# One more pair of the up-projection by Strassen's scheme, and VectorE's taps and Silu product one step later

## The chip, the core and the metric

The kernel runs on one core of a Trainium2 chip (trn2). The metric is the device time of one execution in microseconds (us). Rows of the profile name the engines PE (TensorE's matmuls), PEld (its weight loads), DVE (VectorE), ACT (ScalarE), POOL (GpSimd) and SP (SyncE, which here only issues DMAs).

## The reference

A decoder layer on one sequence of 512 positions and 1024 channels: three mixers (a short convolution, block-sparse causal attention, attention to a fixed memory), a gated merge with a residual add, and then the MLP, in which the change lies:

```python
h2 = rmsnorm(x, g_ffn)
a, b = jnp.split(h2 @ w_up, 2, axis=-1)        # w_up: 1024 x (2 * 2816)
a = causal_dwconv3(a, ffn_conv_w, ffn_conv_b)  # three taps along the positions
x = x + (jax.nn.silu(a) * b) @ w_down
```

All inputs are float32.

## The kernel before

**Tiling.** Channels lie on the partitions in chunks of 128 and the 512 positions along the free axis. Every float32 operand of a matmul is split into a high part (`hi`, rounded by ScalarE) and the rest (`lo`, a subtraction on VectorE), and a product is three matmuls: hi x hi, lo x hi, hi x lo. The weights of the layer are read in pieces of 128 x 1024 in the order of their use.

**The up-projection** makes 22 pairs: columns f and 22 + f of `w_up` give one 128 x 512 block of `a` and one of `b`. Pairs 0 and 1 are made together in 16 steps. A *plain* pair (`plain_pair`, pairs 2 to 5) takes 8 steps of TensorE, each of 6 matmuls of 512 columns. A *fast* pair (`fast_head` and `fast_tail`, pairs 6 to 20, the set `FAST`) multiplies a 2 x 2 arrangement of weight blocks (two column blocks, two halves of the 1024 rows) by a 2 x 2 arrangement of the input (two halves of the rows, two halves of the positions) by Strassen's scheme in the form with fewer sums: 7 products, one step each, of 12 matmuls of 256 columns. The order is head of f (`p6`, `p7`, `p1`, `p5`), tail of f - 1 (`p4`, `p2`, `p3`), head of f + 1, and so on. Pair 21 is plain again and comes outside this list.

A fast pair needs sums of its weights and of the input. The weight sums `sx` are made by VectorE (`sums_1`, `sums_2`, `sums_4`, lines 1199, 1203, 1244), and one of them in place by a GpSimd DMA that adds r2 to r1 (line 1200). The split weights are called `wx` (128 x 1024, of `sx`), `w1` (of r1 after the DMA), `w2` (by DMA, below) and `w4` (128 x 512, of `sx`). The sums of the input (`sum_rows`, split by `sum_split` into the tiles `t`) are made once, at fixed steps ahead of the first fast pair.

**Drains.** The four banks of a pair are called y, z, x and w. ScalarE copies y (`p6_done`, line 1218) and a half of x (`p2_done`, line 1254). VectorE adds from x, z and w (`p1_done`, lines 1222 and 1223; `p5_done`, 1227; `p4_done`, 1250; `p3_done`, 1257). Even pairs use two banks `s` and two banks `m`, odd pairs four banks `acc`, so a bank is written again two pairs later. After `p3_done` come the three taps (`taps_of`): ScalarE the first (line 1074), VectorE the two others (line 1077), ScalarE Silu (line 1081), and VectorE the product with b (`gate_up`, lines 1087 and 1094). Pairs 14 to 17 (`SPILL`) write that product to DRAM by SP.

**Order.** In this stage the order on VectorE, ScalarE, SP and GpSimd is written out: `at(step, job)` puts a job in the list of a step, `later(gen)` runs a generator, one part a step, and every `yield` in it moves the rest to the next step. Jobs of a step run in the order in which they were put there, ahead of the step's matmuls; what drains a product runs behind them. Each engine then works through its own list in order, waiting at each instruction for what that instruction needs. `cut_at` plans a split: `high` at a step h, `low` one step later, h being the first use less a lead (`LEAD`, 7 steps); with `by_dma` ScalarE writes the negated high part as well and two GpSimd DMAs add the weights to it, in place of VectorE's subtraction. Splits go round six places (`place`, `ends`), three in the pool `wp` and three in `fs`; `ends` holds the step of the last use of each place.

Of the kernel before, what the change touches and what calls it, by code (L numbers as in the profile page):

```python
# [25 lines left out]
NWARM = 16  # L26


FAST = frozenset(range(6, 21))


LEAD = 7
# [35 lines left out]
def weight_units():  # L68
# [33 lines left out]
    for f in range(2, NF):  # L102
        if f in FAST:
            for ks in (range(4), range(4, KD)):
# [19 lines left out]
def layer_kernel(ctx: ExitStack, tc: tile.TileContext, xT, memT, vecs, ws, outT):  # L124
# [5 lines left out]
    wp = ctx.enter_context(tc.tile_pool(name="wp", bufs=3))  # L130
# [10 lines left out]
    def nm(s):  # L141
        count[0] += 1
        return f"{s}_{count[0]}"
# [3 lines left out]
    def tmp(n=S, dt=F32):  # L147

        i = tmps[0]
        if i is not None:  # L150
            tmps[0] = (i + 1) % 10
            if i >= 8:
                return cm.tile([P, n], dt, tag="tmp", name=nm("tmp"), bufs=2)
        return tp.tile([P, n], dt, tag="tmp", name=nm("tmp"), bufs=8)
# [3 lines left out]
    def bank(tag="acc"):  # L158
        return ps.tile([P, 512], F32, tag=tag, name=nm(tag), bufs=PSB[tag])
# [97 lines left out]
    def mm3(out, l, r, start, stop):  # L257
        nc.tensor.matmul(out, l[0], r[0], start=start, stop=False)  # L258
        nc.tensor.matmul(out, l[1], r[0], start=False, stop=False)  # L259
        nc.tensor.matmul(out, l[0], r[1], start=False, stop=stop)  # L260
# [14 lines left out]
    def split(dst, src, scale=None):  # L275

        for _ in split_steps(dst, src, scale):
            pass
# [615 lines left out]
    fs = fast.enter_context(tc.tile_pool(name="fs", bufs=1, reuse_waits="tile"))  # L894
# [3 lines left out]
    def taps(f):  # L898
        return [V("f_w", NF * i + f) for i in range(3)], V("f_b", f)
# [16 lines left out]
    def at(i, job):  # L916
        jobs.setdefault(max(i, now[0] + 1), []).append(job)

    def later(gen, wait=1):

        def go():
            if next(gen, "end") is None:
                at(now[0] + 1, go)

        if wait:
            at(now[0] + wait, go)
        else:
            go()
# [4 lines left out]
    base = st["cut"]  # L933
    done = {-1}
    PLACES = 6
    ends = [-1, -1, -1, -1, 3, 7]
    wanted = []
    cutn = [0]
    n_up = 2 * (NF - 2) + 2
# [29 lines left out]
    def place(n):  # L969

        i = cutn[0]
        cutn[0] = i + 1
        pool = fs if i % PLACES in (1, 2, 3) else wp
        return tuple(
            pool.tile([P, 8 * P], FR, tag=t, name=nm(t), bufs=3)[:, :n] for t in ("hi", "lo")
        )
# [35 lines left out]
    def cut_raw(i, first, last, by_dma=False, lead=LEAD):  # L1012
        return cut_at(first, last, lambda: raws[base + i], i, by_dma, lead)
# [9 lines left out]
    def blocks(hl, k, n=1):  # L1023
        return tuple(a[:, k * P : (k + n) * P] for a in hl)
# [45 lines left out]
    def taps_of(f, u, b):  # L1070

        ws, bias = taps(f)
        t = tmp()
        nc.scalar.activation(t, u[:, 0:S], AF.Identity, bias=bias, scale=ws[0])
        yield
        for i in (1, 2):
            nc.vector.scalar_tensor_tensor(
                t, u[:, i : S + i], ws[i], t, op0=ALU.mult, op1=ALU.add
            )
        yield  # L1080
        nc.scalar.activation(t, t, AF.Silu)
        yield
        gate_up(f, b, t)

    def gate_up(f, b, t):
        if f in SPILL:
            nc.vector.tensor_mul(t, b, t)
            nc.sync.dma_start(md[f], t)
            mf[f] = None
            return  # L1090
        n = sum(m is not None for m in mf.values())
        pool, tag = (fm, "mf") if n < NF - 8 - len(SPILL) else (mp, "mj")
        m = pool.tile([P, S], F32, tag=tag, name=nm("mf"))
        nc.vector.tensor_mul(m, b, t)
        mf[f] = m
# [21 lines left out]
    def sum_rows(k):  # L1117

        if k % 2 == 0:
            raw_sums[k] = [tmp() for _ in range(4)]  # L1120
        top, low, c = x2[k], x2[k + KH], slice(H * (k % 2), H * (k % 2) + H)
        t1, t2, t3, t4 = (r[:, c] for r in raw_sums[k & ~1])
        nc.vector.tensor_sub(t1, top[:, H:], top[:, :H])
        nc.vector.tensor_sub(t2, low[:, H:], t1)
        yield
        nc.vector.tensor_sub(t3, low[:, H:], top[:, H:])
        nc.vector.tensor_sub(t4, low[:, :H], t2)

    def sum_split(k, n):
        hl = tuple(fs.tile([P, S], FR, tag="t", name=nm("t"), bufs=16) for _ in range(2))  # L1130
        split(hl, raw_sums[k][n])
        sums[n].extend(tuple(a[:, H * i : H * i + H] for a in hl) for i in range(2))

    for k in range(KH):
        later_at = 24 + 8 * (k // 2) + 2 * (k % 2)
        at(later_at, lambda k=k: later(sum_rows(k), 0))
    for k in range(0, KH, 2):
        for n in range(4):
            at(28 + 4 * k + n, lambda k=k, n=n: sum_split(k, n))

# [3 lines left out]
    def plain_pair(f):  # L1146
        tags = ("acc", "acc") if f % 2 else ("s", "m")
        ws, bias = taps(f)
        box = {}

        def mms(w, h, j):
            def go():
                if j == 0:
                    box[h] = bank(tags[h])
                for k in (2 * j, 2 * j + 1):
                    mm3(box[h], blocks(w, k), hn[k], k == 0, k == KD - 1)

            return go

        def conv():  # L1160
            acc, t = box[0], tmp()
            box["t"] = t
            nc.scalar.activation(t, acc, AF.Identity, bias=bias, scale=ws[2])
            yield
            for i in (1, 2):
                nc.vector.scalar_tensor_tensor(
                    t[:, i:], acc[:, : S - i], ws[2 - i], t[:, i:], op0=ALU.mult, op1=ALU.add
                )
            yield
            nc.scalar.activation(t, t, AF.Silu)  # L1170

        for h in range(2):
            s = len(steps)
            by_dma = f < min(FAST) and (h == 1 or f < 4)
            w = cut_raw(2 * (f - 2) + 2 + h, s, s + 3, by_dma, LEAD + 4 if by_dma else LEAD)
            after = (lambda: later(conv(), 0), lambda: gate_up(f, box[1], box["t"]))[h]
            for j in range(4):
                steps.append((mms(w, h, j), after if j == 3 else None))
# [10 lines left out]
    def fast_head(f):  # L1189
        tags = ("acc",) * 4 if f % 2 else ("s", "m", "s", "m")  # L1190
        s = len(steps)
        i1 = 2 * (f - 2) + 2
        n = KH * P
        q = {}

        def sums_1():
            r1, r2 = raws[base + i1], raws[base + i1 + 1]
            q["sx"] = fs.tile([P, 2 * n], F32, tag="sx", name=nm("sx"), bufs=3)
            nc.vector.tensor_sub(q["sx"][:, n:], r1[:, :n], r1[:, n:])
            nc.gpsimd.dma_start(r1[:, n:], r2[:, n:], accum_op=ALU.add)  # L1200

        def sums_2():
            nc.vector.tensor_sub(q["sx"][:, :n], raws[base + i1 + 1][:, n:], q["sx"][:, n:])

        def sums_at(h):
            at(h - 2, sums_1)
            at(h - 1, sums_2)

        wx = cut_at(s, s + 1, lambda: q["sx"], known=sums_at)
        w1 = cut_raw(i1, s + 2, s + 3, lead=LEAD - 1)  # L1210

        def p6():
            q["y"], q["z"], q["x"], q["w"] = (bank(t) for t in tags)
            q["v"] = tmp()
            product(q["y"], wx, 0, sums[1], True)

        def p6_done():
            nc.scalar.activation(q["v"][:, :H], q["y"][:, :H], AF.Copy)

        def p1_done():  # L1220
            v = q["v"]
            nc.vector.tensor_add(v[:, H:], q["x"][:, :H], v[:, :H])
            nc.vector.tensor_add(v[:, :H], q["z"][:, :H], v[:, H:])

        def p5_done():
            q["b"] = tmp()
            nc.vector.tensor_add(q["b"][:, H:], q["w"][:, :H], q["v"][:, :H])

        steps.extend((
            (p6, p6_done),  # L1230
            (lambda: product(q["z"], wx, KH, sums[2], True), None),
            (lambda: product(q["x"], w1, 0, rows(0, 0), True), p1_done),
            (lambda: product(q["w"], w1, KH, sums[0], True), p5_done),
        ))
        return q
# [31 lines left out]
    for f in range(2, NF - 1):  # L1267
        this = (f, fast_head(f)) if f in FAST else plain_pair(f)
        if tail:
            fast_tail(*tail)  # L1270
        tail = this
    if tail:
        fast_tail(*tail)
    assert NF - 1 not in FAST and cutn[0] == 0
    end = len(steps)
# [17 lines left out]
    i = base + n_up - 2  # L1293
# [19 lines left out]
    for f in range(NF):  # L1313
        pool, tag = (fd, "m") if f < NF - 8 else (hp, "h")
# [83 lines left out]
```

## Time and profile before

| | us |
|---|---|
| median of 3 runs (827.23 to 827.34) | 827.24 |
| the profiled execution | 826.2 |
| its span in the trace | 824.4 |
| TensorE busy | 815.3 |
| VectorE busy | 569.7 |
| ScalarE busy | 436.3 |

The profiled execution took 826.2 us. Its span, from the first instruction of the program to the last, is 824.4; the rest lies around it. Busy time is the union of an engine's instructions. Matmuls overlap in the trace, so the time that one costs is the distance between two starts and not its length. In a timeline a row stands for one instruction, or for several of one kind in a row (x2); the brackets give the idle time of the engine ahead of it and what ended it. TensorE's granted clock is at its upper level (2.4 GHz) in all 40 slices of the profile.

### The profile page before, as it was taken

To read this page: it belongs to the slowest core of one execution; us is meant where nothing else is said; L and a number is where in the kernel's file an instruction comes from. 1 tells how busy PE (TensorE), PEld (TensorE's weight loads), DVE (VectorE), ACT (ScalarE), POOL (GpSimd) and SP (SyncE) were. 2 spreads that over 40 slices of the span, in tenths; PEclk is the share of its full clock that TensorE was granted. 3 is DMA by queue.
4 is the path that set the end of the run, shared out by engine and by line. 5 is a ranking of instruction groups with operands and counts; after the bars stand their busy time and mean duration, and the time that the engine had idled before them with its cause. 6 is when DMAs were issued, how large, how long until landed. Compare 5 with 4: busy or idle time off the path is not lost.

```text
span 824.4 us, 11450 instructions
## 1 busy us (share of the span) xinstructions
PE 815.3 (99%) x4254; PEld 695.0 (84%) x4254; DVE 569.7 (69%) x963; ACT 436.3 (53%) x779; POOL 95.7 (12%) x134
## 2 busy tenths in 40 slices
PE   9999999999999999999999999999999999999998
PEld 7888788888888888888888888899999998888888
DVE  6998898957767777666466587768888888523221
ACT  7676776736655645554334476556656568312210
POOL 0300000101221011110000022222222220000000
PEclk9999999999999999999999999999999999999999
DMA  8453122333332332225334375677777886433310
GB/s 304 131 179 105 58 96 77 117 120 97 118 100 90 107 97 77 80 100 179 102 99 145 126 197 150 156 182 174 180 179 179 206 191 219 140 102 130 113 64 26
DMA packets 38263, 109.08 MB, mean 132 GB/s; under 512 B 4416, under 2 KB 5056, under 8 KB 38080
## 3 DMA queue, kind: packets, MB, share of 16 engines
q1 hardware_dynamic: 29856, 93.34, 33.9%
q0 software_dynamic: 8208, 14.95, 10.6%
q8 instruction: 33, 0.54, 0.3%
q14 instruction: 22, 0.18, 0.1%
q10 hardware_dynamic: 144, 0.08, 0.0%
HBM read 85.01 MB, written 5.24 MB: 109 GB/s over the span
## 4 chain that ended last, share of the span: by engine, by line
PE 77%; DMA 8%; issue 7%; DVE 3%; POOL 3%; ACT 1%; SPq 0%; POOLq 0%; ACTq 0%; DVEq 0%
PE acc L258 19%; PE acc L259 19%; PE acc L260 19%; DMA ra<-raw 5%; PE s L259 4%; PE s L260 4%; PE s L258 4%; POOL lo L993 2%; DMA ra<-rb 2%; PE m L774 1%; PE m L1184 1%; DMA raw<-ws 1%; PE m L260 1%; PE m L259 1%; PE m L258 1%
## 5 line engine op out<-in xcount | busy, mean ns | idle before, releaser
L223 DVE TENSOR_TENSOR lo<-raw,hi 128x1024 fp32r<-128x1024 f32 (+2 forms) x106 | 128.9, 1216 | 126.4 <-ACT hi L220 125.9
L220 ACT ACTIVATE hi<-raw 128x1024 fp32r<-128x1024 f32 (+2 forms) x106 | 110.3, 1041 | 151.1 <-PE acc L260 85.3
L260 PE MATMUL acc<-h,hi 128*128 128x512 f32 x360 | 142.1, 395 | 0.0
L259 PE MATMUL acc<-h,lo 128*128 128x512 f32 x360 | 142.1, 395 | 0.0
L258 PE MATMUL acc<-h,hi 128*128 128x512 f32 x360 | 142.1, 395 | 0.0
L260 PEld LDWEIGHTS acc<-h,hi 128*128 128x128 f32 x360 | 67.7, 188 | 16.1
L259 PEld LDWEIGHTS acc<-h,lo 128*128 128x128 f32 x360 | 67.7, 188 | 15.3
L258 PEld LDWEIGHTS acc<-h,hi 128*128 128x128 f32 x360 | 67.7, 188 | 15.2
L259 PE MATMUL acc<-m,lo 128*128 128x512 f32 (+1 forms) x132 | 47.2, 358 | 0.0
L258 PE MATMUL acc<-m,hi 128*128 128x512 f32 (+1 forms) x132 | 47.2, 358 | 0.0
L260 PE MATMUL acc<-m,hi 128*128 128x512 f32 (+1 forms) x132 | 47.1, 357 | 0.0
L1184 PE MATMUL acc<-t,hi 128*128 128x256 f32 x224 | 43.5, 282 | 0.0
L1184 PE MATMUL m<-t,hi 128*128 128x256 f32 x192 | 38.7, 284 | 1.9 <-DVE tmp L1250 1.9
L986 ACT ACTIVATE hi<-sx 128x1024 fp32r<-128x1024 f32 (+1 forms) x30 | 25.2, 839 | 25.2 <-DVE sx L1244 19.7
L323 ACT ACTIVATE ty<-ty 32x16 f32<-32x16 f32 (+4 forms) x136 | 29.1, 214 | 17.2 <-DVE ty L331 8.2
L1184 PEld LDWEIGHTS acc<-t,hi 128*128 128x128 f32 x224 | 36.1, 190 | 0.0
L1184 PEld LDWEIGHTS m<-t,hi 128*128 128x128 f32 x192 | 31.4, 190 | 2.7 <-DVE tmp L1250 2.7
L720 POOL TENSOR_SCALAR_AFFINE_SELECT S<-S 128x128 f32<-128x128 f32 x32 | 13.0, 415 | 168.4 <-ACT S L718 167.8
L993 POOL DMA_DIRECT2D lo<-raw x28 | 24.5, 1028 | 67.8 <-ACT lo L990 67.8
L1184 PE MATMUL acc<-hn,hi 128*128 128x256 f32 x168 | 32.3, 282 | 0.0
L1184 PE MATMUL acc<-t,lo 128*128 128x256 f32 x112 | 31.6, 282 | 0.0
L802 ACT ACTIVATE tmp<-acc,half_b 128x512 f32<-128x512 f32 x21 | 14.5, 688 | 29.9 <-PE acc L260 29.8
(308 smaller groups left out, 2050.1 us busy)
## 6 DMA issues: line engine op xcount, KB each, us to landing
raw<-ws SPq DMA_DIRECT2D x120, 512.0 KB, 3.3
ra<-ws SPq DMA_DIRECT2D x20, 512.0 KB, 4.0
lo<-raw POOLq DMA_DIRECT2D x28, 256.0 KB, 4.3
ra<-raw POOLq DMA_DIRECT2D x11, 256.0 KB, 5.4
rb<-ws SPq DMA_DIRECT2D x5, 512.0 KB, 4.8
lo<-rb POOLq DMA_DIRECT2D x10, 256.0 KB, 4.3
xr<-xT SPq DMA_DIRECT2D x8, 256.0 KB, 5.6
xres<-xT SPq DMA_DIRECT2D x1, 2048.0 KB, 9.6
```

The source lines that it names most:

```text
L220: nc.scalar.activation(hi[:, :m], raw[:, :m], AF.Copy)
L223: nc.vector.tensor_sub(lo[:, :m], raw[:, :m], hi[:, :m].bitcast(F32))
L258: nc.tensor.matmul(out, l[0], r[0], start=start, stop=False)
L259: nc.tensor.matmul(out, l[1], r[0], start=False, stop=False)
L260: nc.tensor.matmul(out, l[0], r[1], start=False, stop=stop)
L323: nc.scalar.activation(dst, src, AF.Copy)
L720: nc.gpsimd.affine_select(dg, dg, pattern=[[1, P]], compare_op=ALU.is_ge, fill=NEG, base=0, channel_multiplier=-1,)
L774: nc.tensor.matmul(acc[:, i0:], l, b[:, : S - i0], start=i == 0 and b is x[0], stop=i == 3 and b is x[1],)
L802: nc.scalar.activation(z, acc, AF.Tanh, bias=half_b[:, i : i + 1], scale=0.5)
L986: nc.scalar.activation(out[0], a, AF.Copy)
L993: nc.gpsimd.dma_start(out[1][:, c], a[:, c], accum_op=ALU.add)
L1184: nc.tensor.matmul(out[:, :H], a, b, start=first and k == 0 and x == 0, stop=k == KH - 1 and x == 2, skip_group_check=not first,)
```

## The change

Pair 5 joins the set `FAST`. Only pairs 2 to 4 stay plain, the fast part starts at step 40 and not 48, and the whole list has 152 steps and not 153. For that the sums of the input move: `sum_rows` to steps 22, 24, 28 and 30 (before 24, 26, 32, 34), and the splits to 27 to 30 and 33 to 36 (before 28 to 31 and 36 to 39). Of the plain pieces, the first of pair 2 is no longer split by DMA but by VectorE (high part at step 9, low part at step 10). The first three of the six places now lie in `wp` and the others in `fs`, with the last uses in `ends` set to match. In `taps_of` two more `yield` stand: one ahead of VectorE's taps and one ahead of the product.

```diff
-FAST = frozenset(range(6, 21))
+FAST = frozenset(range(5, 21))
...
-    ends = [-1, -1, -1, -1, 3, 7]
+    ends = [-1, 3, 7, -1, -1, -1]
...
-        pool = fs if i % PLACES in (1, 2, 3) else wp
+        pool = wp if i % PLACES < 3 else fs
...
         t = tmp()
         nc.scalar.activation(t, u[:, 0:S], AF.Identity, bias=bias, scale=ws[0])
         yield
+        yield
         for i in (1, 2):
             nc.vector.scalar_tensor_tensor(
                 t, u[:, i : S + i], ws[i], t, op0=ALU.mult, op1=ALU.add
             )
         yield
         nc.scalar.activation(t, t, AF.Silu)
+        yield
         yield
         gate_up(f, b, t)
...
-        later_at = 24 + 8 * (k // 2) + 2 * (k % 2)
+        later_at = 22 + 6 * (k // 2) + 2 * (k % 2)
         at(later_at, lambda k=k: later(sum_rows(k), 0))
...
-            at(28 + 4 * k + n, lambda k=k, n=n: sum_split(k, n))
+            at(27 + 3 * k + n, lambda k=k, n=n: sum_split(k, n))
...
-            by_dma = f < min(FAST) and (h == 1 or f < 4)
+            by_dma = f < min(FAST) and (h == 1 or f == 3)
```

From the written order, VectorE's list between two `p3_done` reads as follows (pair numbers left out; what moves stands in capitals):

```text
before: p3_done, lo of w4, TAPS, lo of wx, PRODUCT, p1_done (2), p5_done, lo of w1, sums_4, p4_done, sums_1, sums_2
after:  p3_done, lo of w4, lo of wx, TAPS, p1_done (2), p5_done, lo of w1, sums_4, PRODUCT, p4_done, sums_1, sums_2
```

ScalarE's list is the same in both: hi of w4, first tap, hi of wx, p6_done, hi and negated hi of w2, Silu, hi of w1, p2_done.

## Rows read from the trace of the kernel before

**Rows 1.** The page, part 1: busy us (share), instructions, by engine.

```profile
PE 815.3 (99%) x4254; PEld 695.0 (84%) x4254; DVE 569.7 (69%) x963; ACT 436.3 (53%) x779; POOL 95.7 (12%) x134
```

**Rows 2.** TensorE's waits (up-projection's): line, waited for, us in total, times, longest.

```profile
PE m L1184 <- DVE tmp L1250: 1.9, 4, 1.0
```

**Rows 3.** TensorE's timeline: start us, length us, engine, line, instruction, [idle before <-releaser].

```profile
522.35 0.39 PE L258 MATMUL acc<-hn,hi 128*128 128x512 f32 x1
...
533.24 0.29 PE L1184 MATMUL s<-t,hi 128*128 128x256 f32 x1
...
559.04 0.28 PE L1184 MATMUL acc<-t,hi 128*128 128x256 f32 x1
...
579.12 0.28 PE L1184 MATMUL acc<-t,hi 128*128 128x256 f32 x1
...
606.28 0.28 PE L1184 MATMUL s<-hn,hi 128*128 128x256 f32 x1
...
611.03 0.38 PE L1184 MATMUL m<-t,hi 128*128 128x256 f32 x1 [0.28 <-DVE tmp L1250]
...
686.49 0.39 PE L258 MATMUL s<-hn,hi 128*128 128x512 f32 x1
```

**Rows 4.** VectorE's timeline, from one `p3_done` to the next.

```profile
601.91 0.42 DVE L1257 TENSOR_TENSOR u<-acc,tmp 128x256 f32<-128x256 f32 x1
602.24 0.68 DVE L998 TENSOR_TENSOR lo<-sx,hi 128x512 fp32r<-128x512 f32 x1
603.27 1.54 DVE L1077 SCALAR_TENSOR_TENSOR tmp<-u,vec,tmp 128x512 f32<-128x512 f32 x2 [0.35 <-ACT tmp L1074]
604.72 1.22 DVE L998 TENSOR_TENSOR lo<-sx,hi 128x1024 fp32r<-128x1024 f32 x1
606.89 0.69 DVE L1094 TENSOR_TENSOR mf<-tmp,tmp 128x512 f32<-128x512 f32 x1 [0.95 <-ACT tmp L1081]
607.50 0.42 DVE L1222 TENSOR_TENSOR tmp<-acc,tmp 128x256 f32<-128x256 f32 x1
607.95 0.42 DVE L1223 TENSOR_TENSOR tmp<-acc,tmp 128x256 f32<-128x256 f32 x1
608.48 0.42 DVE L1227 TENSOR_TENSOR tmp<-acc,tmp 128x256 f32<-128x256 f32 x1
608.82 1.22 DVE L998 TENSOR_TENSOR lo<-ra,hi 128x1024 fp32r<-128x1024 f32 x1
609.95 0.69 DVE L1244 TENSOR_TENSOR sx<-raw,sx 128x512 f32<-128x512 f32 x1
610.56 0.42 DVE L1250 TENSOR_TENSOR tmp<-m,tmp 128x256 f32<-128x256 f32 x1
610.89 0.68 DVE L1199 TENSOR_TENSOR sx<-ra 128x512 f32<-128x512 f32 x1
611.61 0.69 DVE L1203 TENSOR_TENSOR sx<-raw,sx 128x512 f32<-128x512 f32 x1
612.21 0.42 DVE L1257 TENSOR_TENSOR u<-m,tmp 128x256 f32<-128x256 f32 x1
```

**Rows 5.** Busy us from 512 to 534: PE, PEld, DVE, ACT, POOL; clock, DMA, GB/s.

```profile
512.00:534.00 22.00, 22.00 (x101) 18.21 (x100) 17.11 (x27) 12.54 (x17) 4.09 (x6) 1.00 0.49 117
```

**Rows 6.** DMA issues: out<-in, queue, count, KB each, median us to landing.

```profile
ra<-raw POOLq DMA_DIRECT2D x11, 256.0 KB, 5.4
```

**Rows 7.** Timelines of ScalarE and GpSimd beside rows 4.

```profile
602.42 0.82 ACT L1074 ACTIVATE tmp<-u,vec 128x512 f32<-128x512 f32 x1 [1.42 <-DVE u L1257]
603.14 1.04 ACT L986 ACTIVATE hi<-sx 128x1024 fp32r<-128x1024 f32 x1
606.24 0.62 ACT L1081 ACTIVATE tmp<-tmp 128x512 f32<-128x512 f32 x1
606.76 1.05 ACT L986 ACTIVATE hi<-ra 128x1024 fp32r<-128x1024 f32 x1
...
601.56 0.86 POOL L1200 DMA_DIRECT2D ra<-rb  x1 [3.49 <-DVE sx L1199]
```

## The prediction

> **What bounds the kernel now.** I read the engine totals first: TensorE is busy 815.3 of 824.4 us [rows 1]. A busy TensorE is the bound as long as nobody makes it wait, so the next view is the list of its waits, and that has one entry behind the stage that the change touches: four waits for VectorE's add at line 1250, 1.9 us in all [rows 2]. That add (`p4_done`) is the last reader of bank `z` of a fast pair, and product `p7` of the pair two later writes the same bank.
>
> The third view, TensorE's timeline, gives the price of the two kinds of pair [rows 3]. Plain pair 5 lasts from 522.35 to 533.24, 10.89 us. Two fast pairs without a wait, from the first product of pair 9 to that of pair 11 (559.04 to 579.12), are 20.08 us: 10.04 a pair, 1.434 a product. The whole fast part, 105 products from 533.24 to 686.49, takes 153.25 us where 105 x 1.434 is 150.6. So 2.65 us are lost there. The waits and the slow restart behind each are that loss.
>
> The fourth view says why VectorE is late. Its timeline from one `p3_done` to the next (601.91 to 612.21) is its whole order for one pair [rows 4]: 10.30 us against TensorE's 10.04. It isn't waiting for TensorE: its only two idle times are 0.35 ahead of the taps and 0.95 ahead of the Silu product, both for ScalarE. So it falls behind by 10.30 - 10.04 = 0.26 us a pair until its add at line 1250 holds up TensorE. That add began at 610.56, 4.28 us after product `p4` of its pair ended (606.28, where the next product begins), and TensorE stood 0.28 us for it at 611.03 [rows 3, 4]. I therefore put the lag that TensorE can bear at 4.28 - 0.28 = 4.0 us.
>
> **The change part by part.** *Pair 5.* 48 matmuls of 512 columns (8 steps) become 84 of 256 (7 products): 10.89 us become 10.04, **-0.85** [rows 3]. A rule speaks against it. The rows show about 0.227 us for a matmul of 512 columns (10.89/48) and 0.1195 for one of 256 (1.434/12): half the columns at little over half the time. The Trainium skill ("TensorE: Matmul & The Clock Gate", section "Back-to-back issue gap") states that in a stream of weight load and matmul pairs one of 512 columns takes about 131 ns and one of 128 about 81. By that, as an estimate, 84 matmuls between those figures (6.8 to 11.0 us) would replace 48 (6.3 us) and the pair would grow by 0.5 to 4.7 us. The measured spacing decides, and that rule gets no chance.
>
> *What moves ahead of the fast part.* Pair 5 now begins at step 40, not 48. The row sums and their splits go from steps 24 to 39 into 22 to 36; piece 2 loses ScalarE's negated copy and two GpSimd DMAs and gets a VectorE subtraction at step 10 (SP's loads of pieces 6 and 7 follow at 10 instead of 5, and are first read at 25); the places for the split weights change pool. Piece 2 is needed at step 16, six steps later. VectorE was busy 17.11 of the 22 us from 512 to 534 [rows 5], so it has 4.9 us of cover there, and TensorE has no wait there at all [rows 2]. I cost this at 0. If the cover is gone, pair 5's `w2`, which lands by GpSimd's DMA, or its sums come late. The DMA that adds r2 to r1 has a median of 5.4 us from issue to landing [rows 6]; a lateness of a fifth of that, 1 us, is my upper bound. Below 0 there is nothing to gain, because TensorE doesn't wait there.
>
> *The taps and the product one step later.* This is the part that decides. In VectorE's order of one pair the taps move behind the low half of `wx`, and the product moves from ahead of `p1_done` to just ahead of `p4_done`. On ScalarE nothing changes place: first value of the taps (line 1074), high half of `wx`, ..., Silu, high half of `w1` [rows 7]. I follow both engines from the start of `p3_done` (0):
> - ScalarE's line 1074 starts at 0.51 (602.42 - 601.91), the high half of `wx` at 1.23 and it ends at 2.27 (603.14 + 1.04) [rows 7]. VectorE starts 0.03 us after a ScalarE result (602.42 + 0.82 = 603.24, taps at 603.27).
> - Before, VectorE spends that time in the taps, and the low half of `wx` at 2.81 waits for nothing. After, that low half is next behind the low half of `w4`, which ends at 1.01: it waits until 2.30, **1.29 us in place of 0.35**. The taps, queued behind it, run from 3.43 (1.13 later, 608.82 to 609.95 for the same shape) to 4.97, and VectorE is free at 4.88 (1.45 for the two).
> - Silu needs the taps: 4.97 + 0.09 (the 0.51 less the add's 0.42) is 5.06. The high half of `w1` follows 0.52 later (606.24 to 606.76), at 5.58, and ends at 6.63. Before it started at 4.85.
> - VectorE's `p1_done` and `p5_done` take 0.45 + 0.53 + 0.34 from 4.88 and end at 6.20. They are behind TensorE's `p1`, which ends at 3 x 1.434 = 4.30, so they wait for nothing. The low half of `w1` wants to start at 6.20 and must wait for 6.66: **0.46 us that was not there**.
> - Then 1.13 (low half), 0.61 (line 1244), 0.61 (product, whose Silu ended at 5.68: its wait of 0.95 is gone), 0.33 (line 1250, started at 9.01), 0.72, 0.60: the next `p3_done` at **10.66**.
>
> So 1.30 us of idle time become 1.75: VectorE loses 10.66 - 10.04 = 0.62 us a pair where it lost 0.26. Queued behind each wait are all drains of the banks, and TensorE waits for the one at line 1250.
>
> *The loss after.* Pair 6 is the first whose `p4_done` stands behind a full turn. With `p3_done` of pair 5 0.3 us after its product, the lag is 0.3 + 9.01 - 5 x 1.434 = 2.14. Up to pair 18, the last whose bank is wanted again, 12 turns add 12 x 0.62 = 7.4. That is 9.6 in all, and 4.0 is borne: **5.6 us lost**. The same working for before gives 0.3 + 8.65 - 7.17 + 11 x 0.26 - 4.0 = 0.6, and 2.65 was measured; 2.0 us come from events outside the regular turn. The likeliest is the DMA into r1: its median of 5.4 us [rows 6] is longer than the 5.2 us that the turn gives it (issued at 601.56, 0.35 ahead of `p3_done`, and wanted at 4.85) [rows 7]. After the change it is wanted 0.73 later, but VectorE then has no slack behind it. So 0 to 2.0 more; I take the middle, 1.0. Loss after 6.6 (5.6 to 7.6), less 2.65: **+3.95** (2.95 to 4.95).
>
> *SP's queue.* In pairs 14 to 17 the product issues a write to DRAM. It moves from ahead of the two weight loads that wait for the low half of `w1` to behind them; the loads lose a wait, and nobody reads that write before the down-projection: 0.
>
> *The end of the stage.* The last pairs have no pair behind them and their order is the same; pair 21 and the down-projection follow as before: 0.
>
> **Sum:** -0.85 + 3.95 = +3.1 us (2.1 to 4.1, with a late start 5.1). The profiled run took 826.2 (span 824.4), the median is 827.24, 1.0 higher; I put the difference on the median: **830.3**, between 829.3 and 832.3.
>
> **The rivals.** *VectorE is relieved* (faster). The product no longer waits for Silu, and if the high half of `wx` were ready when the low half of `w4` ends, a turn would cost 10.30 - 1.30 = 9.00 us, under 10.04. TensorE would then wait for nothing: -0.85 - 2.65 = -3.5, 823.7. For it: 1.30 us of each turn are such waits [rows 4]. It decides if that high half is ready at 1.0 us. Against it: ScalarE stood 1.42 us for `p3_done` itself [rows 7], so the high half can't start until line 1074 is done. 0.08.
>
> *Only the first new wait comes.* If the high half of `w1` isn't held by Silu, the turn is 10.20, the add at line 1250 lies at 8.55 and the lag reaches 0.3 + 8.55 - 7.17 + 12 x 0.16 = 3.6: under 4.0, and only the irregular 1 us or so remains. -0.85 - 1.65 = -2.5, 824.7. Against it: Silu can't start before the taps end. 0.07.
>
> *The order makes no difference*, the turn stays 10.30 and one fast pair more adds 0.26 to the loss: -0.6, 826.6. For it: two waits go, two come, nearly equal. 0.13.
>
> *The start is late as well*: +1 on the forecast, 831.3; it lies inside its range. 0.06 of the forecast's 0.72.
>
> **How the numbers follow.** Forecast 0.72. A comparison of this kernel tells 0.2% (1.65 us) from no change, so slower begins at 828.9, below the forecast's own range. A small part of the forecast may still fall under it: slower 0.71, same 0.14, faster 0.15. The range takes in the forecast to its upper bound and the rival of no difference: 826.0 to 832.5; the two faster rivals (0.15) and the tail lie outside.
>
> **What would show it.** In the new profile VectorE's low half of `wx` should carry an idle time near 1.3 us for ScalarE, the low half of `w1` one near 0.4, the Silu product none, and `p3_done` should come every 10.6 to 10.9 us. TensorE's waits for line 1250 should begin by pair 11, come in odd and even pairs, about 0.6 us each, and sum to 5 us or more. Forecast and arithmetic fall if the turn is under 10.04 us or if the waits have gone. Step 40 without a wait would bear out the cost of 0 for the moved sums.

## The result, and the profile after

The changed kernel takes 833.45 us (median of 5 runs, 832.62 to 834.75) where the kernel before takes 827.33 (827.23 to 827.48): ratio 1.0086, 95% interval 1.0072 to 1.0099. It is slower by 6.1 us; 3.1 were forecast, and the time lies above the range. (The ratios here are those on record for the runs; the quotient of these two medians alone is 1.0074.) The profiled execution took 832.62 (span 830.8), 6.4 more than that of before.

Two lines are added, so line numbers are 1 higher from the taps and 2 higher from the product on (`p4_done` is line 1252, `p3_done` 1259, a fast matmul 1186). TensorE's timeline cuts the span into four stretches (columns as in [rows 3]):

```profile
468.01 0.40 PE L258 MATMUL acc<-h,hi 128*128 128x512 f32 x1
...
523.53 0.28 PE L1186 MATMUL acc<-t,hi 128*128 128x256 f32 x1
...
594.67 0.39 PE L1186 MATMUL m<-t,hi 128*128 128x256 f32 x1 [0.99 <-DVE tmp L1252]
...
692.92 0.39 PE L258 MATMUL s<-hn,hi 128*128 128x512 f32 x1
```

The first row is the first matmul of the up-projection, the second the first fast product, the third one of TensorE's waits, the last the first matmul of pair 21. The same four stretches of before begin at 0, here:

```profile
466.95 0.40 PE L258 MATMUL acc<-h,hi 128*128 128x512 f32 x1
```

and at 533.24 and 686.49 [rows 3]. So the plain steps take 55.52 us (before 66.29), the fast part 169.39 (before 153.25), and what follows 137.9 in both. Of the fast part 112 x 1.434 = 160.6 are products; 8.78 are lost, where 2.68 were. The sum is -10.77 + 16.14 = +5.4 us in the stage that was changed. The missing 1.06 lie ahead of it (466.95 against 468.01), in code that is the same in both. In the 14 other profiles of this study that stretch ends anywhere from 466.3 to 468.2, also between versions that differ only behind it. A row of TensorE's waits there is an example, after:

```profile
PE s L259 <- DVE lo L223: 1.2, 1, 1.2
```

and the same row before:

```profile
PE s L259 <- DVE lo L223: 0.5, 1, 0.5
```

So this 1 us is spread between executions, and the table below compares the changed stage alone.

TensorE's waits in the up-projection, the view of [rows 2]: seven for `p4_done` in place of four, 7.3 us in place of 1.9. The columns behind the colon are us in total, times, and the longest.

```profile
PE m L1186 <- DVE tmp L1252: 7.3, 7, 1.2
```

VectorE's timeline of one *turn* (from one `p3_done` to the next), the view of [rows 4]:

```profile
585.22 0.42 DVE L1259 TENSOR_TENSOR u<-acc,tmp 128x256 f32<-128x256 f32 x1
585.55 0.68 DVE L998 TENSOR_TENSOR lo<-sx,hi 128x512 fp32r<-128x512 f32 x1
587.53 1.23 DVE L998 TENSOR_TENSOR lo<-sx,hi 128x1024 fp32r<-128x1024 f32 x1 [1.29 <-ACT hi L986]
588.67 1.53 DVE L1078 SCALAR_TENSOR_TENSOR tmp<-u,vec,tmp 128x512 f32<-128x512 f32 x2
...
591.10 0.42 DVE L1229 TENSOR_TENSOR tmp<-acc,tmp 128x256 f32<-128x256 f32 x1
591.85 1.22 DVE L998 TENSOR_TENSOR lo<-ra,hi 128x1024 fp32r<-128x1024 f32 x1 [0.32 <-ACT hi L986]
592.99 0.68 DVE L1246 TENSOR_TENSOR sx<-raw,sx 128x512 f32<-128x512 f32 x1
593.59 0.68 DVE L1096 TENSOR_TENSOR mf<-tmp,tmp 128x512 f32<-128x512 f32 x1
594.19 0.42 DVE L1252 TENSOR_TENSOR tmp<-m,tmp 128x256 f32<-128x256 f32 x1
...
595.85 0.42 DVE L1259 TENSOR_TENSOR u<-m,tmp 128x256 f32<-128x256 f32 x1
```

and of ScalarE beside it, the view of [rows 7]:

```profile
585.73 0.82 ACT L1074 ACTIVATE tmp<-u,vec 128x512 f32<-128x512 f32 x1 [2.02 <-DVE u L1259]
586.45 1.04 ACT L986 ACTIVATE hi<-sx 128x1024 fp32r<-128x1024 f32 x1
...
590.23 0.63 ACT L1082 ACTIVATE tmp<-tmp 128x512 f32<-128x512 f32 x1 [0.58 <-DVE tmp L1078]
590.77 1.04 ACT L986 ACTIVATE hi<-ra 128x1024 fp32r<-128x1024 f32 x1
```

The low half of `wx` waits 1.29 us, the low half of `w1` 0.32, the product not at all, and the turn is 595.85 - 585.22 = 10.63 us (10.64 on most pairs). Forecast were 1.29, 0.46 and 10.66. The turn is what was worked out; the loss must come from elsewhere. It begins before the first full turn. This is how VectorE comes into the fast part, after (timeline of all engines):

```profile
521.54 1.54 DVE L1168 SCALAR_TENSOR_TENSOR tmp<-s,vec,tmp 128x511 f32<-128x511 f32 x2
522.99 1.22 DVE L998 TENSOR_TENSOR lo<-ra,hi 128x1024 fp32r<-128x1024 f32 x1
...
524.23 0.33 SPq L958 DMA_DIRECT2D ra<-ws  x1
...
529.76 0.86 POOL L1202 DMA_DIRECT2D ra<-raw  x1 [2.02 <-DVE tmp L1224]
...
538.15 1.06 ACT L986 ACTIVATE hi<-ra 128x1024 fp32r<-128x1024 f32 x1 [4.33 <-PE acc L1186]
...
539.25 1.23 DVE L998 TENSOR_TENSOR lo<-ra,hi 128x1024 fp32r<-128x1024 f32 x1 [3.65 <-ACT hi L986]
539.26 0.28 PE L1186 MATMUL acc<-t,hi 128*128 128x256 f32 x1
...
542.65 0.42 DVE L1259 TENSOR_TENSOR u<-acc,tmp 128x256 f32<-128x256 f32 x1
```

and before:

```profile
530.25 1.22 DVE L998 TENSOR_TENSOR lo<-ra,hi 128x1024 fp32r<-128x1024 f32 x1
...
531.50 0.33 SPq L958 DMA_DIRECT2D ra<-ws  x1
...
537.20 0.86 POOL L1200 DMA_DIRECT2D ra<-raw  x1 [2.08 <-DMA raw<-ws]
...
546.35 1.22 DVE L998 TENSOR_TENSOR lo<-ra,hi 128x1024 fp32r<-128x1024 f32 x1 [0.98 <-ACT hi L986]
...
549.07 0.28 PE L1184 MATMUL s<-t,hi 128*128 128x256 f32 x1
...
549.75 0.42 DVE L1257 TENSOR_TENSOR u<-m,tmp 128x256 f32<-128x256 f32 x1
```

The first `p3_done` starts 542.65 - 539.26 = 3.39 us behind the end of its product, before 549.75 - 549.07 = 0.68. I call this the *entry lag*. Followed back, counted from the first fast product (523.53; before 533.24): VectorE waited 3.65 us (before 0.98) for the high half of the third fast pair's `w1`. That needs the DMA that adds r2 to r1, issued 6.23 us in (before 3.96) and landed 8.2 us later (before 7.9): at 537.99, 0.16 ahead of ScalarE's row, which the view puts down to a matmul long done. The DMA is issued 0.56 us behind the landing of r2, the second of the loads that SP issued 0.70 in (before 1.74 *ahead*). These start as soon as the low half of the first fast pair's `w1` has ended (522.99 + 1.22 = 524.21), and that began 0.54 ahead (before 2.99 ahead). VectorE, whose order is packed there, comes to it 2.45 us later than before. So of the 2.60 us by which that DMA lands later, 2.27 are its later issue and 0.33 its transfer, which was long in before too.

VectorE's share of the 22 us ahead of the fast part (third of the busy times, the view of [rows 5]), after:

```profile
501.50:523.50 22.00, 22.00 (x97) 18.07 (x96) 20.54 (x39) 13.04 (x19) 3.46 (x4) 1.00 0.57 123
```

and before:

```profile
511.27:533.24 21.97, 21.97 (x98) 18.04 (x97) 17.34 (x28) 12.51 (x17) 3.47 (x4) 1.00 0.49 111
```

It is busy 20.54 us there, not 17.34.

That landing sets the entry lag in every version. In eleven of the twelve versions with pair 5 fast (the changed kernel and those of the table below) the lag is the landing, counted from the first fast product, less 11.07 or 11.08 us; in the three with pair 5 plain it is the landing less 11.18. The twelfth is the one with the sums 2 steps earlier: there TensorE itself waits 0.66 us ahead of the entry, and it is the landing less 11.99.

### The profile page after: what moved, and what is told of

Its sections match the earlier page's. It is cut to its first block, busy times and chain, and to the rows that moved or that the text cites. A ratio compares the mean times of both kernels' runs of the same rounds, so it can differ in the third digit from the quotient of the medians.

```text
span 830.8 us, 11553 instructions
## 1 busy us (share of the span) xinstructions
PE 814.2 (98%) x4290; PEld 695.0 (84%) x4290; DVE 576.7 (69%) x974; ACT 438.0 (53%) x782; POOL 94.1 (11%) x133
## 4 chain that ended last, share of the span: by engine, by line
PE 72%; DVE 14%; ACT 5%; issue 5%; DMA 3%; SPq 0%; POOL 0%; DVEq 0%; ACTq 0%; POOLq 0%
PE acc L260 19%; PE acc L258 19%; PE acc L259 19%; PE s L259 4%; ACT hi L986 3%; PE s L260 3%; PE s L258 3%; DVE lo L998 2%; DVE tmp L1078 2%; DMA raw<-ws 2%; PE m L774 1%; DVE sx L1246 1%; DVE sx L1201 1%; DMA ra<-raw 1%; DVE sx L1205 1%
## 5 line engine op out<-in xcount | busy, mean ns | idle before, releaser
L1186 PE MATMUL acc<-t,hi 128*128 128x256 f32 x256 | 49.7, 282 | 0.0
L998 DVE TENSOR_TENSOR lo<-sx,hi 128x1024 fp32r<-128x1024 f32 (+1 forms) x32 | 30.5, 953 | 17.1 <-ACT hi L986 17.1
L1186 PEld LDWEIGHTS acc<-t,hi 128*128 128x128 f32 x256 | 41.2, 190 | 0.0
L1186 PE MATMUL acc<-hn,hi 128*128 128x256 f32 x192 | 36.9, 282 | 0.0
L1186 PE MATMUL acc<-t,lo 128*128 128x256 f32 x128 | 36.1, 282 | 0.0
```

The source lines that it names most:

```text
L998: nc.vector.tensor_sub(out[1], src(), out[0].bitcast(F32))
L1186: nc.tensor.matmul(out[:, :H], a, b, start=first and k == 0 and x == 0, stop=k == KH - 1 and x == 2, skip_group_check=not first,)
```

## The experiments

One table holds what the profiles of all versions show (us): the fast part's loss (its length less 1.434 a product), the entry lag, VectorE's usual turn, the plain steps and the fast part together less those of before (219.53), and the measured ratio to the kernel before on the same chip. "Pair only" is the changed kernel without the two new `yield` (some expectations call these turns as well). A loss a little under 0 says that 1.434 a product is slightly high for that profile.

| version | lost | entry lag | turn | stage less before | ratio, 95% interval |
|---|---|---|---|---|---|
| before | 2.68 | 0.68 | 10.32 | 0 | |
| changed kernel | 8.78 | 3.39 | 10.64 | +5.4 | 1.0086 (1.0072 to 1.0099) |
| order only | 6.35 | 0.24 | 10.64 | +3.7 | 1.0037 (1.0023 to 1.0052) |
| pair only | 6.40 | 4.35 | 10.31 | +3.0 | 1.0021 (1.0011 to 1.0031) |
| pair, taps late | 2.94 | 2.99 | 10.04, one of 11.5 | -0.5 | 1.0006 (0.9992 to 1.0020) |
| pair, product late | 0.42 | 3.44 | 9.4, some to 11.4 | -3.0 | 0.9972 (0.9960 to 0.9983) |
| before, product late | 0.17 | 0.98 | 9.4, some to 11.2 | -2.5 | 0.9981 (0.9969 to 0.9993) |
| pair, first tap and product late | 3.86 | 4.18 | 9.6, some to 12.8 | +0.5 | 0.9983 (0.9971 to 0.9996) |
| pair only, sums 2 steps earlier | 6.62 | 3.50 | 10.31 | +3.2 | 1.0032 (1.0018 to 1.0046) |
| pair only, taps of pair 4 late | 3.93 | 1.94 | 10.31 | +0.5 | 1.0011 (1.0001 to 1.0021) |
| pair only, no DMAs of `w2` | 2.57 | 0.66 | 10.31 | -0.8 | 0.9998 (0.9986 to 1.0010) |
| changed, no DMAs of `w2` | 7.20 | 1.19 | 10.64 | +3.8 | 1.0043 (1.0028 to 1.0058) |
| changed, taps of pair 4 late | 8.08 | 1.85 | 10.64 | +4.7 | 1.0060 (1.0043 to 1.0077) |
| first tap, product late, sums 1 earlier | 0.99 | 3.45 | 9.6, some to 11 | -2.4 | 0.9958 (0.9945 to 0.9972) |
| the same, taps of pair 4 late | -0.31 | 1.98 | 9.6, some to 11.2 | -3.7 | 0.9959 (0.9940 to 0.9979) |

My theory was that the order costs by the turn and the late entry on top of it; the rivals were that one of the two does it alone.

**The two parts of the change, one at a time.** *Pair only*, the order as before:

```diff
         yield
-        yield
         for i in (1, 2):
...
-        yield
         yield
         gate_up(f, b, t)
```

> The changed kernel with both new yields taken out: pair 5 fast, sums and splits moved, taps and product where they were. Theory (VectorE's turn and its lag at entry add up): the turn is 10.30 us again; it enters some 3 us late as in the changed kernel (p3_done of pair 5 3.39 us after its product), so the lag at line 1250 would reach 3.39 + 8.65 - 7.17 + 12 x 0.26 = 8.0, of which 4.0 is borne: 4.0 us lost, +0.5 against before, about 827.8. Rival 1 (the late entry alone is the cause, the order costs nothing): as slow as the change, 832 to 834. Rival 2 (the order is all, the entry costs nothing): loss as before plus 0.26, about 826.7.

*Order only*: the kernel before with these two `yield` put in.

> The kernel before with the two new yields alone: pair 5 plain, sums in their old place. Theory: the turn is 10.64 us, with 1.29 us of waiting ahead of the low half of wx and 0.32 ahead of that of w1; from the lag of p3_done of pair 6 (0.68) line 1250 reaches 0.68 + 9.01 - 7.17 + 11 x 0.60 = 9.1, so 5.1 us are lost where 2.65 were: +2.5, about 829.8. Rival 1 (the late entry alone): 827.3. Rival 2 (order is all): 831 to 833.

Pair only took 829.27 us, order only 830.59, the kernel before 827.0 beside them. Each part is slower by itself. Order only has the long turn and an early entry (0.24): its loss grows by 3.67. Pair only has the old turn, and its loss grows by 3.72 with an entry lag that grew by 3.67. The prediction's sum had the second at nothing, and the expectation of this run had it too small: it took the changed kernel's lag of 3.39 and no late landing, 0.5 us over the kernel before, where 2.3 were measured.

**The order, one `yield` at a time.** *Pair, product late*: only the `yield` ahead of the taps goes.

> The changed kernel without the yield ahead of VectorE's taps: only the product comes one step later. Theory: the wait for Silu (0.95) goes, the taps stay ahead of wx; by the rows of before the low half of w1 then waits 0.67 for its high half and the turn is 9.93 us, under TensorE's 10.04. VectorE enters 3 us late, holds there and gains 0.1 a pair; TensorE waits some 1 to 1.5 us in all: about 824.7 (824 to 826). If it is as slow as the change (over 831), the turn is not what decides.

*Pair, taps late*: only the `yield` ahead of the product goes.

> The changed kernel without the yield ahead of the product: only the taps come one step later, so the product stands between p1_done and p5_done. Theory: the wait for the high half of wx is there (1.3), and the product fills most of the time in which w1's high half is made, so the turn is 10.20 us: 3.39 + 8.55 - 7.17 + 12 x 0.16 = 6.7, 2.7 lost, about 826.5. The rival that both shifts cost alike puts it midway between the change and the kernel without them, about 830.

*Before, product late*: the kernel before with the `yield` ahead of the product alone.

> The kernel before with the product alone one step later (pair 5 plain, sums and taps in their old place). Theory: a turn of 9.35 to 9.95 us (the wait for Silu goes, late landings of the DMA into r1 put some of it back), under TensorE's 10.04, so nothing of the 2.7 us is lost: 2.5 us under before, ratio 0.997. With e3 it says what pair 5 is worth by itself: e3 should lie 0.4 to 0.9 lower. Rival (e3's gain was pair 5's): ratio 1.000.

They took 824.56, 827.23 and 824.27 us. The product one step later is what helps, with pair 5 or without it (between these two the stage differs by 0.5 us for pair 5): it then stands behind `p1_done`, and its wait for Silu is 0.17 and not 0.95 [rows 4]. VectorE's timeline with the product late:

```profile
586.15 0.69 DVE L1095 TENSOR_TENSOR mf<-tmp,tmp 128x512 f32<-128x512 f32 x1 [0.17 <-ACT tmp L1081]
...
598.52 1.22 DVE L998 TENSOR_TENSOR lo<-ra,hi 128x1024 fp32r<-128x1024 f32 x1 [1.97 <-ACT hi L986]
```

A turn without other waits is 9.4 us there, under TensorE's 10.04. VectorE catches up until the r2-to-r1 DMA holds it (the second row), which costs TensorE nearly nothing. An entry lag of 3.44 us is then free, too. With the taps late alone:

```profile
583.27 1.23 DVE L998 TENSOR_TENSOR lo<-sx,hi 128x1024 fp32r<-128x1024 f32 x1 [1.29 <-ACT hi L986]
...
586.66 0.68 DVE L1095 TENSOR_TENSOR mf<-tmp,tmp 128x512 f32<-128x512 f32 x1
...
587.60 1.23 DVE L998 TENSOR_TENSOR lo<-ra,hi 128x1024 fp32r<-128x1024 f32 x1
```

The wait for `wx` is there (1.29), but the product, with 0.60 to the instruction behind it, fills the time in which VectorE would wait for the high half of `w1`. Counted from its `p3_done`, the low half of `w1` starts at 6.63 us in this version (587.60 - 580.97) and in the changed kernel (591.85 - 585.22). The changed kernel still has the product's 0.60 to do behind it: that is its 10.64 against 10.04 here.

**Why the taps must not stand behind `wx`.** ScalarE makes the high half of `wx` only behind the first tap, which needs `p3_done`. *Pair, first tap and product late*: the first tap goes behind that high half as well.

```diff
-            later(taps_of(f, q["u"], q["b"]), 0)
+            later(taps_of(f, q["u"], q["b"]), 1)
...
         yield
-        yield
         for i in (1, 2):
```

> The changed kernel with VectorE's order kept (low half of wx, then taps; product late) but the first tap on ScalarE one step later too, so that ScalarE makes the high half of wx first and doesn't wait for p3_done ahead of it; the extra yield ahead of VectorE's taps goes. Theory: what cost in the change was the wait for that high half behind the first tap, not the order on VectorE; the wait of 1.29 falls to about 0.3, the turn to 9.6 to 9.9 us, the loss to under 1: 824 to 825. Rival (taps behind wx cost by themselves): as the change, over 831.

It took 825.34 us, and the wait is gone down to 0.19:

```profile
583.60 1.22 DVE L998 TENSOR_TENSOR lo<-sx,hi 128x1024 fp32r<-128x1024 f32 x1 [0.19 <-ACT hi L986]
```

So ScalarE's place for the tap made that wait. The loss of 3.86 was expected under 1. The profile of this version has one r2-to-r1 DMA late in the stage that landed after 7.95 us; VectorE waits 3.56 us behind it, and TensorE's longest wait, 1.5 of 2.7 us in all, follows.

**Why the entry is late.** First guess: too many sums in VectorE's order ahead of the fast part. *Pair only, sums 2 steps earlier*:

```diff
-        later_at = 22 + 6 * (k // 2) + 2 * (k % 2)
+        later_at = 20 + 6 * (k // 2) + 2 * (k % 2)
...
-            at(27 + 3 * k + n, lambda k=k, n=n: sum_split(k, n))
+            at(25 + 3 * k + n, lambda k=k, n=n: sum_split(k, n))
```

> The kernel of e1 (pair 5 fast, taps and product in their old place) with the row sums and their splits two steps earlier (from step 20 and 25). What it asks is why VectorE enters the fast part 4.35 us late there. Theory (crowding: eight splits and sixteen sums in too few steps make w1 of pair 5, the loads behind it and the DMA that adds r2 to r1 of pair 7 late): two steps are 2.8 us, the lag at entry falls to 1.5 to 2.2 and the loss of the fast part from 6.4 to about 3.9, 2.5 us less than e1. Rival (that DMA is slow by itself, 8 to 9.5 us from issue to landing whatever stands ahead of it, and its issue hangs on nothing that the sums delay): the lag stays over 4 and the time stays that of e1.

It failed: 828.89 us, entry lag 3.50, and that only because TensorE waits ahead of the entry; the DMA lands 15.49 us in, where pair only has 15.42. The low half of `w1` of pair 5 came no earlier. Second guess: the chain from that low half over SP's loads to the DMA, or else the DMA itself. *Pair only, taps of pair 4 late*, in `conv` of the plain pairs:

```diff
             nc.scalar.activation(t, acc, AF.Identity, bias=bias, scale=ws[2])
             yield
+            if f == min(FAST) - 1:
+                yield
             for i in (1, 2):
```

> The changed kernel without both turns (the second-tap and product order as in the kernel before), and with VectorE's two taps of pair 4, the last plain pair, one step later in its order, so that the low half of w1 of pair 5 is made ahead of them. Theory A (the late entry is a chain: the low half of w1 of pair 5 ends late, so the loads of pieces 12 and 13 start late, so r1 += r2 of pair 7 starts late, and VectorE waits for the high half made from it): the low half of w1 comes about 1.4 us earlier, and the loads and r1 += r2 with it; the entry lag of the first fast pair falls from 4.35 us to about 2.9, the loss from 6.4 to about 5, and the time is 1.4 us below that of the version without the turns (829.3), about 827.9. Theory B (r1 += r2 of pair 7 is late because its transfer is slow, whatever starts it): the entry stays at 4.3 and the time at 829.3.

*Pair only, no DMAs of `w2`* of pair 5, in the split by DMA (this version leaves out a term of that low half, so its result is not the layer's):

```diff
-            for c in range(0, n, 4 * P):
+            for c in range(0, n if raw != 2 * (min(FAST) - 2) + 3 else 0, 4 * P):
```

> The changed kernel without both turns, and without the two GpSimd DMAs that add the low part's second term to the low half of w2 of pair 5 (that low part then lacks this term: it is left out). These two are in flight beside r1 += r2 of pair 7. Theory B (r1 += r2 of pair 7 takes 8 to 9.5 us because of what shares GpSimd's DMA queue with it): it lands in 4 to 5 us, the entry lag falls from 4.35 to about 1 us, the loss from 6.4 to about 3, the time to about 826. Theory A (its transfer is slow beside the loads of the pieces, or its start is late): its landing stays near 8 us, and entry and time stay as in the version without the turns (4.35 us, 829.3 us).

The first took 827.66 us, the second 826.17 (before beside them 826.50). VectorE's timeline with the taps of pair 4 late; the low half of `w1` now stands ahead of them, and the later wait is 2.21 where it is 4.62 in pair only:

```profile
521.39 1.22 DVE L998 TENSOR_TENSOR lo<-ra,hi 128x1024 fp32r<-128x1024 f32 x1
522.52 1.53 DVE L1168 SCALAR_TENSOR_TENSOR tmp<-s,vec,tmp 128x511 f32<-128x511 f32 x2
...
537.65 1.22 DVE L998 TENSOR_TENSOR lo<-ra,hi 128x1024 fp32r<-128x1024 f32 x1 [2.21 <-ACT hi L986]
```

The entry lag falls by 2.41, the loss by 2.47. The chain is there, but it is the smaller part of this gain: the low half of `w1` starts 1.45 us sooner and the loads 1.44, the DMA into r1 is issued only 0.62 sooner, and it then lands in 7.7 us and not 9.5. That is also why the gain is larger than the 1.4 expected. Without the two DMAs of `w2` the DMA into r1 is issued no sooner, but it lands in 5.6 us, and the entry lag is 0.66. The DMA part of the page, in the same 14.8 us from SP's loads on, of pair only (packets, MB, share of 16 engines):

```profile
DMA  0095999999999999997976975989999999999953
q0 software_dynamic: 682, 1.25, 48.8%
q1 hardware_dynamic: 576, 2.10, 44.6%
```

and without the two DMAs:

```profile
DMA  0029799999303898599899994210003999699958
q0 software_dynamic: 432, 0.79, 30.7%
q1 hardware_dynamic: 588, 2.15, 40.4%
```

In pair only the 16 DMA engines are busy without a gap once the loads have begun, with 4 loads of 512 KB and 5 additions of 256 KB issued, and all but the first ones land late. So both guesses hold in part: a late start, and a transfer that then shares the engines with four loads and the halves of `w2`. The Trainium skill ("DMA: Bandwidth & Descriptors", section "Issuing engines are not separate DMA queues") states that transfers run on the same 16 engines and interleave whichever engine started them; these rows agree: taking two of GpSimd's away let SP's loads of pieces 14 and 15 land in 3.4 and 4.5 us where they took 7.7 and 9.9. The DMA into r1 also stands behind the two halves of `w2` in GpSimd's own queue; whether that order or the shared engines hold it up more, no run here tells apart.

**Do turn and entry add?** The same two edits on the changed kernel.

> The changed kernel, with both turns of the order, without the two GpSimd DMAs that complete the low half of w2 of pair 5 (this term is left out). Theory (the cost of the change is the longer turn of VectorE, 10.64 us against TensorE's 10.04, and on top of it the late entry into the fast part, and the two add): the transfer r1 += r2 of pair 7 lands about 3 us sooner, the entry lag falls from 3.39 us to about 0.7, the turn stays 10.64, the loss falls from 8.78 to about 6.1 us and the time from 833.4 to about 830.7, ratio 1.004 to 1.006: what was forecast with an entry of 0.3. Rival (the late entry is taken up by the cover anyway, the order alone makes the loss): the loss stays at 8.8 and the ratio at 1.0075 to 1.0095.

> The changed kernel, with both turns of the order, and with VectorE's two taps of pair 4 one step later. Theory (turn and entry add): as in the version without the turns, where this edit took 2.41 us from the entry lag and 2.47 from the loss, it takes here most of 2.4 us from the entry (3.39 to about 1.0) and from the loss (8.8 to about 6.4): time about 831, ratio 1.004 to 1.006. Rival (the order alone makes the loss): ratio stays at 1.0075 to 1.0095 and the loss at 8.8.

They took 829.84 and 831.18 us (before 826.05), so the time falls with the entry while the turn stays 10.64. Their losses, 7.20 and 8.08, are above the 6.1 and 6.4 expected, for two reasons that the profiles show: the entry lag fell to 1.19 and 1.85 only, and each has longer turns late in the stage (10.92 and 11.15 in the first, 11.63 in the second), which the profile of the changed kernel has not. The wait behind that of the second, 1.32 where 0.32 is usual:

```profile
665.89 1.22 DVE L998 TENSOR_TENSOR lo<-ra,hi 128x1024 fp32r<-128x1024 f32 x1 [1.32 <-ACT hi L986]
```

With each profile's own entry lag and its own turns, long ones included (twelve, or eleven where pair 5 is plain; 8.65 for 9.01 with the old order), the prediction's loss formula gives 7.0 and 7.9 for these two. In the same way it gives 8.6 for the changed kernel, 6.1 for pair only, 3.7 and 2.4 for its versions with the taps late and without the DMAs, and 2.4 for the kernel before: 0.2 to 0.3 under the measured loss in all seven. (In order only it gives 5.4 of 6.35, with the sums 2 steps earlier 5.5 of 6.62.) So turn and entry add. By time the first version lies clear of the changed kernel; the interval of the second (1.0043 to 1.0077) still touches that of the changed kernel (1.0072 to 1.0099).

**A version that is faster than both.** *First tap and product late, sums one step earlier* (21 and 26 in place of 22 and 27), and *the same with the taps of pair 4 late*:

> e5 with the sums and splits one step earlier (from step 21 and 26). Theory: lag at entry lower by about 1.4 us, but with a turn under 10.04 us the entry is borne anyway: the loss is 0 to 0.4, so about 3.3 us under before (ratio 0.996), within 0.5 us of e5 and e3.

> The version with the first tap on ScalarE one step later, the product one step later and the sums one step earlier (ratio 0.9958), and VectorE's two taps of pair 4 one step later too. Its turn of VectorE is about 10.0 us on the mean, just under the 10.04 of TensorE, so the entry lag is within the four microseconds of cover: both theories give the same time as without the edit, ratio 0.995 to 0.997; a loss would come only if the later taps of pair 4 hold up TensorE's plain steps.

They took 823.89 and 822.60 us (before 826.89 and 826.50 beside them), ratios 0.9958 and 0.9959. In the second, TensorE waits for VectorE nowhere in the fast part.

## Why the prediction was wrong in size

**The order: right.** The turn (10.66 forecast, 10.64 measured), both new waits and the product without one came as forecast. The waits of TensorE did not come as named, in odd and even pairs and 0.6 us each: all seven are for a bank `m`, so of even pairs alone, and 1.0 to 1.2 us long. The four of before were for `m` as well [rows 2]. In order only, where nothing else is changed, the loss grew by 3.67; the step gave 11 x 0.62 against 11 x 0.26, 4.0. The rivals of a relieved VectorE, of the first wait alone and of no difference fall with the turn. The rival of a late start was right in kind, with a price far too small.

**The moved sums and the early start: wrong.** This is the step that failed: "I cost this at 0", with 1 us as the upper bound, and in the loss formula "`p3_done` of pair 5 0.3 us after its product". It started 3.39 us after. With 3.39 for 0.3 and the measured 0.60 for the excess of a turn the same formula gives 3.39 + 9.01 - 7.17 + 12 x 0.60 - 4.0 = 8.4; 8.78 were measured. The reasoning failed at three places. The 4.9 us of cover were those of VectorE's average before; with eight plain steps fewer to hold the moved sums and the fast part's own order, 1.5 us were left. TensorE "has no wait there at all" was true before and after and says nothing: the first wait of the changed kernel comes at 552.1. For the same reason step 40 without a wait, named as the sign that would bear out the cost of 0, did come and bore out nothing. An engine that enters late owes that time, and with a turn longer than TensorE's it never earns it back, so beyond the 4.0 us that are borne every microsecond of entry lag is one of time (pair only: 3.67 of lag, 3.72 of loss; taps of pair 4 late: 2.41 and 2.47 back). And as bound I took a fifth of a landing, where a chain of VectorE, SP, a load and a DMA was late as a whole. Which of the moved work makes VectorE come to that chain 2.45 us later stays open: the sums two steps earlier didn't bring the low half of `w1` forward, and the taps of pair 4 behind it did, by 1.45.

**The irregular part.** I took 1.0 (0 to 2.0). With its own entry lag and usual turn in the formula, before has about 1.5 beyond it, order only 1.7, pair only 1.3, the changed kernel in its profile 0.4 and without the DMAs of `w2` 1.0. The size was fair; the executions differ, and the profiled one is the fastest of the five of the changed kernel. Most of it, in order only about half, is single longer turns. The two of before, 10.88 and 10.94 us, are those whose DMA into r1 landed after 6.66 and 6.72 us; VectorE's low half of `w1` waited 0.47 and 0.53 for ScalarE there, and not at all in the turn of [rows 4]. That bears out the cause named for it; in other versions not every long turn was followed back.

**Pair 5 itself** was worth 10.77 - 10.04 = 0.73 (forecast 0.85): its row of 10.89 was saved, but the steps ahead of it take 0.12 more (55.52, where before has 522.35 - 466.95 = 55.40). SP's moved write and the end of the stage: 0, as forecast (137.9 us in both).

**The sum.** -0.73 + 6.10 = +5.4 in the stage. The medians differ by 6.1; the 0.7 between lie within the spread of the stretch ahead of it, and what makes that spread wasn't tried.

## What to carry to other kernels

Where a loop's engine has a longer turn than the bound, the state in which it enters the loop counts as much as the turn: look for its lag behind TensorE at the entry, not for waits of TensorE there. When work is moved behind an instruction that waits, ask which other engine's order makes that wait, and move the piece that fills it last: here one of the two moves alone helped (0.9972), and together they lost. Work put ahead of a loop is to be followed to the DMAs that it lets start.

## What the runs showed of the hardware that I had not expected

The addition by DMA is dear in the DMA engines' time. In the rows above GpSimd's queue, which here carries additions alone, takes 0.488 x 16 x 14.8 / 1.25 = 92 us of engine time per MB (and 92 without the DMAs of `w2`: 0.307 x 16 x 14.8 / 0.79), SP's loads 50 and 45. So the two halves of `w2`, 0.5 MB, hold all 16 engines for about 3 us (an estimate from these rows, and rather an upper one, since the times of packets can overlap: in a view of 2 us of before the two queues' shares add up to 108.6%). One addition of 256 KB landed in 3.25 us with no load in flight (before, issued at 528.15), and in 7.9 (before), 8.2 (changed kernel) and 9.5 us (pair only) with four loads and other additions beside it.
